# A transformer step with a two-way scan: row transfers by halves, operand loads two items ahead, side jobs in more slots

## The chip, the cores and the metric

The kernel runs on one core of one Trainium2 chip. The metric is device time in microseconds (us) of one execution; a kernel's number is the median of its runs.

## What is computed

One layer on 128 context and 1024 latent tokens, 1024 channels: a half-step SwiGLU FFN, a token mixer, a second half-step FFN, each between norms with modulation. The mixer is what the change touches. Its first branch is a scan over tokens in both directions, for 8 heads of 64 channels:

```python
kk = k_h * p['k_k'].astype(f32).reshape(H, N)
kk = kk * lax.rsqrt(jnp.sum(kk * kk, -1, keepdims=True) + 1e-12)
...
k_d = k_h * (1 + (a_d - 1) * k_a)
...
S = (S * w_t[:, :, None, :]
     + sa[..., None] * (kk_t * a_t)[:, :, None, :]
     + v_t[..., None] * k_t[:, :, None, :])
...
y = y + ((bonus[0] + bonus[1]) * v_h).reshape(B, T, D_RWKV)
y = y * jax.nn.sigmoid(g.astype(f32))
```

The second branch is a gated convolution of width 3. Both are projected, gated, added and projected again.

## The kernel before, in words

Channels lie on the 128 partitions, tokens along the free axis, in three tiles of 384 tokens. A dense product is three matmuls of 128x384 (high and low halves of a split float32), lines L740 to L742, tile `pj`; a projection of 128 output channels over all tokens is 24 products. The mixer has 1056 products.

A pair of heads shares 128 partitions and is called p (0 to 3). Its projections r, k and v, and per direction the decay `sg` and two iclr factors, go to DRAM: `opd`, nine rows per pair, with a view `ops2` of two pairs. What the scan needs of a pair's two heads stands in mirrored rows: `mirrored` (L772) writes or reads head 0 at one row and head 1 at the next, as one transfer whose first dimension is 2. `k_to_dram` stores k so, `stage_k` loads and stores so.

The scan is cut into 18 items: (g, j) with two groups g of two pairs and eight blocks j of 128 tokens for latent tokens, then two items for the context. An item covers block j forwards and block 7 - j backwards. `front` calls `stage_b` once per direction: it loads the decays into `SG` (one buffer per direction) and five operand rows into `ops` (pool `q2`, two buffers), multiplies them on VectorE and GpSimd, and makes the products `scr` (L1043) and `bkt` (L1058) on TensorE. `solve` inverts a triangular matrix, on VectorE for the most part, and ends in the matmuls `l` (L1112). `seq_latent` runs the scan's two steps (`sq`, `yp`).

Beside the items run side jobs in three lanes, at most one step of one of them every second slot: `stage_k` makes kk (matmuls `cps`, `kkb`, `bon`), stores it, and stores the bonus to `bvd`; `stage_v` turns v (`vt`); `finish` ends y (`gv`) and stores it to `yad`. A slot is one dense product; a job says with `yield n` how many slots it lets pass. `PB.first` sets an instruction behind the product of its slot in the scheduler's order. `fill(n)` passes n slots, and `need` passes slots until a job is done. The loop over items is:

```python
            if i + 1 < NI:
                gn, jn = items[i + 1]
                need("kk", *((jn, -1) if gn == 2 else (gn, jn // 2, 3 - jn // 2)))
            with chain():
                if i + 1 < NI:
                    front(i + 1)
                ...
                if i + 1 < NI:
                    solve(A[i + 1], i + 1)
            side(jobs.get(i, ()))
            fill(GI)
```

`chain` gives an item's instructions the highest priority, `beside` gives the side jobs the next, and the products the lowest; from these priorities and its own estimate of times a scheduler sets each engine's order, which the chip then keeps. All transfers but one are issued by SP in order. What waits for kk: item 0 for blocks 0 and 3 of group 0, item 2 for blocks 1 and 2, items 8 and 10 for the same of group 1, items 16 and 17 for the context.

Of the kernel before, what the change touches and what calls it, by code (L numbers as in the profile page):

```python
# [658 lines left out]
def mixer(nc, tc, pool, env):  # L659
# [49 lines left out]
    def store(dst, src):  # L709

        late.append((dst, src, clock["dense"]))
# [59 lines left out]

    def mirrored(p, row, sign, t0, n):  # L772

        t_ = ops2[p // 2]
        ps = 18 * T
        return bass.AP(tensor=t_.tensor, offset=t_.offset + 2 * row * T + p % 2 * T + t0, ap=[[64 * ps + 2 * sign * T, 2], [ps, 64], [1, n]])

    def k_to_dram(p):
        def f(t, ps):
            o = e.tmp("fso", tag="s")  # L780
            PB.first(S.activation(out=o, in_=ps, func=AF.Copy))
            store(mirrored(p, 5, -1, t * TW, TW), o)
        return f

    made = set()
# [14 lines left out]
    with ExitStack() as ph:  # L800
# [15 lines left out]
            G.memset(t_, 0.0)  # L816
        HR = [slice(0, 64), slice(64, 128)]

        GI, GF, GL, GM, GC, SG_ = 40, 8, 16, 6, 14, 2
        def job_g(p):  # L820
            yield from proj(1536 + p * 128, to_dram(gd[p], AF.Tanh, scale=0.5))
            evict()
# [120 lines left out]
        def stage_k(p, t0, n, bon=True):  # L943

            while ("rkv", p) not in made:
                yield 1
            nt = n // 128
            k = q1.tile([128, 256], F32, name="ok", tag="ok")[:, :n]
            PB.first(SP.dma_start(k, mirrored(p, 5, -1, t0, n)))
            r = oload(opd[p][:, 3], t0, n, "or")  # L950
            f0, f1 = (q1.tile([128, 256], F32, name=f"o{x}", tag=f"o{x}")[:, :n] for x in "di")
            SP.dma_start(f0, mirrored(p, 2, -1, t0, n))
            SP.dma_start(f1, mirrored(p, 7, -1, t0, n))
            yield GL
            a = q1.tile([128, 256], F32, name="oa", tag="oa")[:, :n]
            PB.first(S.activation(out=a, in_=k, func=AF.Square, scale=e.KK_[:, p:p + 1]))
            b = f0
            PB.first(V.tensor_tensor(out=b, in0=f0, in1=f1, op=ALU.add))
            V.tensor_tensor(out=b, in0=b, in1=k, op=ALU.mult)
            V.scalar_tensor_tensor(out=b, in0=r, scalar=rk4[:, p:p + 1], in1=b, op0=ALU.mult, op1=ALU.mult)  # L960
            v = r
            SP.dma_start(v, vd[p][:, t0:t0 + n])
            yield 3
            rs = compact(a, nt, sel, 2, 1.0, 1e-12, "oc", PB)
            yield GC
            ps = ps_.tile([128, 256], F32, name="kkb", tag="oc", bufs=1)[:, :n]
            for i in range(nt):
                for h in range(2):
                    PB.matmul(ps[HR[h], i * 128:(i + 1) * 128], rs[:, 2 * i + h:2 * i + h + 1].to_broadcast([128, 64]), ident, start=True, stop=True)
            kk = a  # L970
            V.scalar_tensor_tensor(out=kk, in0=k, scalar=e.KK_[:, p:p + 1], in1=ps, op0=ALU.mult, op1=ALU.mult)
            SP.dma_start(mirrored(p, 4, 1, t0, n), kk)
            made.add(("kk", p, (t0 - NCTX) // 256))
            yield 4
            ps = ps_.tile([128, 256], F32, name="bon", tag="oc", bufs=1)[:, :n]
            PB.matmul(ps, bones, b, start=True, stop=True)
            o = v
            V.tensor_tensor(out=o, in0=v, in1=ps, op=ALU.mult)
            S.activation(out=o, in_=o, func=AF.Identity, bias=gb4[:, p:p + 1])
            SP.dma_start(bvd[p][:, t0:t0 + n], o)  # L980
            yield GF

        def stage_v(p, t0, n, zv):
# [13 lines left out]
                S.activation(out=zv[HR[1 - h], 0:nb, p % 2, HR[h]], in_=ps[HR[1 - h], 0:nb], func=AF.Copy)  # L997
            made.add(("vt", p, (t0 - NCTX) // 256))

        def oload(src, t0, n, tag, first=lambda ins: None):  # L1000
            a = q1.tile([128, 256], F32, name=tag, tag=tag)[:, :n]
            first(SP.dma_start(a, src[:, t0:t0 + n]))
            return a

        def zi(g, b):

            return b if g == 0 else (1, 0, 3, 2)[b]

        def stage_b(g, d, t0, A, it):

            n, nb, s0 = 256, 4, 0
            assert all(("kk", 2 * g + pp, (t0 - NCTX) // 256) in made for pp in range(2))
            ops = q2.tile([128, 5, 256], F32, name="ops", tag="ops")
            sg = SG[d][:, :nb]
            for pp in range(2):
                SP.dma_start(sg[:, 2 * pp:2 * pp + 2, 1:65], ops2[g][:, 8 * d, pp, t0:t0 + 128].rearrange("p (s t) -> p s t", t=64))
            SP.dma_start(ops.rearrange("p k (i t) -> p k i t", i=2), ops2[g][:, 1 + 2 * d:6 + 2 * d, :, t0:t0 + 128])
            X, r, kw = (ops[:, 0:2], ops[:, 2], ops[:, 3:5]) if d == 0 else (ops[:, 3:5], ops[:, 0], ops[:, 1:3])
            c3 = "p (s t) -> p s t"
            Fd = q1.tile([128, 4, 65], F32, name="ff", tag="ff")[:, :nb]  # L1020
# [176 lines left out]
        def item_bufs():  # L1197
            ab = [s2.tile([128, 2, 4, 128], F32, name=f"ab{d}", tag=f"AB{d}") for d in range(2)]
            return {"N": q1.tile([128, 2, 4, 32], F32, name="nn", tag="nn"), "T": [t_[:, 0] for t_ in ab], "BT": [t_[:, 1] for t_ in ab],
                    "FT": [s2.tile([128, 4], F32, name=f"ft{d}", tag=f"FT{d}") for d in range(2)],  # L1200
                    "E": [s2.tile([128, 4, 2, 128], F32, name=f"e{d}", tag=f"S{d}") for d in range(2)]}

        def finish(p, t0, n, y):
            while ("g", p) not in made:
                yield 1
            nt = n // 128
            bv = oload(bvd[p], t0, n, "f1", PB.first)
            tg = oload(gd[p], t0, n, "f2", PB.first)
            yc = q1.tile([128, 256], F32, name="yc_", tag="f3")[:, :n]
            yo = y  # L1210
            if t0 < NCTX:
                ps = ps_.tile([128, 256], F32, name="gm", tag="oc", bufs=1)[:, :n]
                PB.matmul(ps, bones, y, start=True, stop=True)
                V.scalar_tensor_tensor(out=yc, in0=ps, scalar=-1.0 / 64, in1=y, op0=ALU.mult, op1=ALU.add)
                yo = yc
            a = q1.tile([128, 256], F32, name="ysq", tag="f4")[:, :n]
            PB.first(S.activation(out=a, in_=yo, func=AF.Square))
            yield GM
            rs = compact(a, nt, sel, 2, 1.0 / 64, 64e-5, "oc", PB)
            yield GC  # L1220
            ps = ps_.tile([128, 256], F32, name="gv", tag="oc", bufs=1)[:, :n]
            for i in range(nt):
                for h in range(2):
                    PB.matmul(ps[HR[h], i * 128:(i + 1) * 128], rs[:, 2 * i + h:2 * i + h + 1].to_broadcast([128, 64]), ident, start=True, stop=True)
            V.tensor_tensor(out=yc, in0=yo, in1=ps, op=ALU.mult)
            V.scalar_tensor_tensor(out=yc, in0=yc, scalar=gg4[:, p:p + 1], in1=bv, op0=ALU.mult, op1=ALU.add)
            o = tg
            V.scalar_tensor_tensor(out=o, in0=tg, scalar=1.0, in1=yc, op0=ALU.add, op1=ALU.mult)
            SP.dma_start(yad[p][:, t0:t0 + n], o)
            made.add(("y", p, (t0 - NCTX) // 256))  # L1230

        def init_state(p, A):
# [87 lines left out]

        def front(i):
            g, j = items[i]
            A[i] = item_bufs()
            if g < 2:
                stage_b(g, 0, NCTX + j * 128, A[i], i)
                stage_b(g, 1, NCTX + (7 - j) * 128, A[i], i)
            else:
                for d in range(2):
                    stage_b(j, d, 0, A[i], i)
# [71 lines left out]
        def beside():  # L1401
            return tc.high_priority(offset=39000)

        side(ks(0, 0, 3) + vs(0, 0, 3))
        need("kk", 0, 0, 3)
        with chain():
# [2 lines left out]
        for i, (g, j) in enumerate(items):  # L1409
            if g == 1 and j in (0, 2):  # L1410
                need("y", 0, *((1, 2), (0, 3))[j // 2])
            if g < 2 and j in (0, 2):
                need("vt", g, *((0, 3), (1, 2))[j // 2])
            if g == 2:
                need("vt", j, -1)
                need("y", 1, *((1,), (2,))[j])
            if i + 1 < NI:
                gn, jn = items[i + 1]
                need("kk", *((jn, -1) if gn == 2 else (gn, jn // 2, 3 - jn // 2)))
            with chain():  # L1420
                if i + 1 < NI:
                    front(i + 1)
                if g < 2:
                    seq_latent(g, j, A[i], A.get(i + 1) if j < 7 else None)
                else:
                    seq_ctx(j, A[i])
                if i + 1 < NI:
                    solve(A[i + 1], i + 1)
            side(jobs.get(i, ()))
            fill(GI)  # L1430
        while any(l.cur for l in lanes.values()):
            fill(1)

# [85 lines left out]
```

## Time and profile before

| | us |
|---|---|
| median of 3 runs | 3277.09 |
| lowest, highest | 3270.9, 3281.26 |
| the profiled execution | 3285.59 |
| its span, first to last instruction | 3283.8 |
| PE busy | 3023.5 (92%) |
| VectorE (DVE) busy | 1817.5 (55%) |
| ScalarE (ACT) busy | 1150.9 (35%) |
| GpSimd (POOL) busy | 454.6 (14%) |
| bytes moved by DMA | 330.78 MB, 101 GB/s over the span |

The span in 40 slices of 82 us, in tenths; the mixer lies in slices 12 to 27:

```profile
PE   8999999999989878888889898769989999999998
DVE  7535665565875244557674667766683233323356
PEclk9999999999989988988999889869999999999999
```

A row names engine, tile and line. "Idle before" is the time that the engine had nothing to do before the instruction, and behind the arrow stands what ended it. PEclk is the granted clock of TensorE as a share of 2.4 GHz; it has two levels, 1.2 and 2.4 GHz, so 0.75 over a stretch means that half of it ran at 1.2.

### The profile page before, as it was taken

The page shows a single profiled execution, that of the slowest core. Times are in us where ns is not written, and L with a number is a line of the kernel's source. Part 1 is how long each engine was busy: PE and PEld are TensorE (multiplying, and loading weights), DVE is VectorE, ACT ScalarE, POOL GpSimd, SP SyncE. Part 2 cuts the span into 40 slices and gives each one's busy share as a digit, 9 for nine tenths or more (in the row PEclk, how much of TensorE's full clock was granted, in tenths as well). Part 3 has the DMA queues.
Part 4 walks back from the last instruction along what each step waited for, and adds up shares of the span by engine and source line. Part 5 has one row for each costly group of instructions (what it writes and reads, how often), then busy time and mean ns, then how long its engine had stood idle before and what let it go on. Part 6 is the DMA issues. An engine that isn't in the chain of part 4 may idle for free.

```text
span 3283.8 us, 54891 instructions
## 1 busy us (share of the span) xinstructions
PE 3023.5 (92%) x21284; PEld 2850.2 (87%) x21284; DVE 1817.5 (55%) x4148; ACT 1150.9 (35%) x2618; POOL 454.6 (14%) x436
## 2 busy tenths in 40 slices
PE   8999999999989878888889898769989999999998
PEld 5999999999888867767777777649989999999998
DVE  7535665565875244557674667766683233323356
ACT  5421111114546224344544444422554211121244
POOL 1000000000240121333331323200120000000012
PEclk9999999999989988988999889869999999999999
DMA  8423333325534331322232333225532111111244
GB/s 270 144 63 95 97 102 87 86 85 153 157 109 162 125 118 58 110 76 78 81 111 84 98 87 98 85 78 157 178 104 87 36 46 43 44 39 42 82 144 132
DMA packets 481137, 330.78 MB, mean 101 GB/s; under 512 B 47008, under 2 KB 458988, under 8 KB 480876
## 3 DMA queue, kind: packets, MB, share of 16 engines
q1 hardware_dynamic: 480248, 326.79, 33.4%
q8 instruction: 167, 2.74, 0.3%
q14 instruction: 94, 0.77, 0.1%
q10 hardware_dynamic: 308, 0.44, 0.0%
q0 software_dynamic: 320, 0.04, 0.0%
HBM read 265.58 MB, written 61.60 MB: 100 GB/s over the span
## 4 chain that ended last, share of the span: by engine, by line
PE 68%; DVE 17%; DMA 6%; ACT 4%; issue 3%; POOL 1%; SPq 0%; DVEq 0%; ACTq 0%; POOLq 0%
PE po L220 6%; PE po L219 6%; PE po L221 6%; PE pg L220 5%; PE pg L219 5%; PE pg L221 5%; PE pu L220 5%; PE pu L219 5%; PE pu L221 5%; PE pj L740 3%; PE pj L742 2%; PE pj L741 2%; DVE un L1084 2%; PE scr L1043 2%; DMA ops<-opd 2%
## 5 line engine op out<-in xcount | busy, mean ns | idle before, releaser
L138 ACT ACTIVATE whi<-wst 128x512 fp32r<-128x512 f32 (+1 forms) x578 | 350.4, 611 | 753.1 <-PE po L221 392.8
L139 DVE TENSOR_TENSOR wlo<-wst,whi 128x512 fp32r<-128x512 f32 (+1 forms) x480 | 326.6, 681 | 305.2 <-ACT whi L138 295.7
L740 PE MATMUL pj<-hh,wlo 128*128 128x384 f32 x1056 | 382.2, 362 | 0.3 <-ACT fso L768 0.3
L741 PE MATMUL pj<-hl,whi 128*128 128x384 f32 x1056 | 372.7, 353 | 2.7 <-POOL hl L269 1.4
L742 PE MATMUL pj<-hh,whi 128*128 128x384 f32 x1056 | 374.6, 355 | 0.0
L219 PE MATMUL po<-ah,wlo 128*128 128x384 f32 x1056 | 357.1, 339 | 4.0 <-ACT ah L138 4.0
L220 PE MATMUL pg<-hl,whi 128*128 128x384 f32 x1056 | 356.1, 337 | 4.9 <-POOL hl L269 2.9
L219 PE MATMUL pg<-hh,wlo 128*128 128x384 f32 x1056 | 357.4, 338 | 1.7 <-DVE wlo L139 1.3
L220 PE MATMUL po<-al,whi 128*128 128x384 f32 x1056 | 356.3, 338 | 0.4 <-DVE al L139 0.4
L221 PE MATMUL po<-ah,whi 128*128 128x384 f32 x1056 | 355.7, 337 | 0.0
L221 PE MATMUL pg<-hh,whi 128*128 128x384 f32 x1056 | 355.5, 337 | 0.0
L219 PE MATMUL pu<-hh,wlo 128*128 128x384 f32 x1056 | 355.2, 336 | 0.0
L220 PE MATMUL pu<-hl,whi 128*128 128x384 f32 x1056 | 353.8, 335 | 0.0
L221 PE MATMUL pu<-hh,whi 128*128 128x384 f32 x1056 | 353.8, 335 | 0.0
L279 POOL TENSOR_TENSOR ss<-ss,sqt 128x384 f32<-128x384 f32 x78 | 88.7, 1140 | 1697.0 <-ACT sqt L278 1534.9
L432 DVE TENSOR_TENSOR sil<-sil,pu 128x384 f32<-128x384 f32 x132 | 72.9, 552 | 353.8 <-PE pu L221 353.6
L404 DVE TENSOR_TENSOR o<-o,po 128x384 f32<-128x384 f32 x288 | 159.2, 553 | 172.0 <-PE po L221 170.8
L740 PEld LDWEIGHTS pj<-hh,wlo 128*128 128x128 f32 x1056 | 206.4, 195 | 12.5 <-issue 7.0
L741 PEld LDWEIGHTS pj<-hl,whi 128*128 128x128 f32 x1056 | 207.1, 196 | 8.6 <-issue 2.2
L742 PEld LDWEIGHTS pj<-hh,whi 128*128 128x128 f32 x1056 | 206.9, 196 | 7.6 <-issue 3.7
L220 PEld LDWEIGHTS pg<-hl,whi 128*128 128x128 f32 x1056 | 199.9, 189 | 7.0 <-POOL hl L269 3.8
L219 PEld LDWEIGHTS po<-ah,wlo 128*128 128x128 f32 x1056 | 198.6, 188 | 5.0 <-ACT ah L138 5.0
(584 smaller groups left out, 5763.9 us busy)
## 6 DMA issues: line engine op xcount, KB each, us to landing
wst<-in_ffn_w SPq DMA_DIRECT2D x324, 256.0 KB
wmod<-in_w_mod SPq DMA_DIRECT2D x144, 256.0 KB
wst<-in_w_in SPq DMA_DIRECT2D x94, 256.0 KB
ops<-opd SPq DMA_DIRECT2D x36, 640.0 KB
wst<-in_ffn_w SPq DMA_DIRECT2D x96, 192.0 KB
xo<-xd SPq DMA_DIRECT2D x64, 192.0 KB
wst<-in_w_out SPq DMA_DIRECT2D x48, 256.0 KB
opd<-zv SPq DMA_DIRECT2D x24, 384.0 KB
```

Source lines behind the costliest of these rows:

```text
L138: first(S.activation(out=hi, in_=src, func=AF.Copy))
L139: eng.tensor_tensor(out=lo, in0=src, in1=hi.bitcast(F32), op=ALU.subtract)
L219: PE.matmul(ps, lo, xh, start=(k == 0), stop=False)
L220: PE.matmul(ps, hi, xl, start=False, stop=False)
L221: later.tick(PE.matmul(ps, hi, xh, start=False, stop=(k == nk - 1)))
L279: eng.tensor_tensor(out=ssum, in0=ssum, in1=q, op=ALU.add)
L404: V.tensor_tensor(out=O[m][t], in0=O[m][t], in1=ps, op=ALU.add)
L432: V.tensor_tensor(out=s, in0=s, in1=pu, op=ALU.mult)
L740: PE.matmul(ps, lo, xh, start=(k == 0), stop=False)
L741: PE.matmul(ps, hi, xl, start=False, stop=False)
L742: ins = PE.matmul(ps, hi, xh, start=False, stop=(k == 7))
L1043: PE.matmul(ps[64 * o:64 * o + 64, i], BK[64 * h:64 * h + 64, o, i * 64:i * 64 + 64], E[64 * h:64 * h + 64, s0 + i, h], start=True, stop=True)
```

## The change

Four edits. `mirrored` gives two transfers of 64 rows, and its users issue both. `stage_k` marks its loads and stores with the product of their slot, and passes slots in other places: 4 before kk's store, 4 before the bonus's, where it passed 4 in one place, so 49 in all instead of 45; `finish` passes 4 before its store. The operand loads move from `stage_b` to `operands(i)`, which is called for item i + 2 after 16 of the 40 slots of item i, if kk is there by then, and from `front` otherwise. The slots of `fill(GI)` become `GO` = 16 and the rest.

```diff
     def mirrored(p, row, sign, t0, n):
 
-        t_ = ops2[p // 2]
-        ps = 18 * T
-        return bass.AP(tensor=t_.tensor, offset=t_.offset + 2 * row * T + p % 2 * T + t0, ap=[[64 * ps + 2 * sign * T, 2], [ps, 64], [1, n]])
+        return [opd[p][64 * h:64 * h + 64, row + sign * h, t0:t0 + n] for h in range(2)]
...
-            store(mirrored(p, 5, -1, t * TW, TW), o)
+            for h, dst in enumerate(mirrored(p, 5, -1, t * TW, TW)):
+                store(dst, o[64 * h:64 * h + 64])
...
-            PB.first(SP.dma_start(k, mirrored(p, 5, -1, t0, n)))
-            r = oload(opd[p][:, 3], t0, n, "or")
+            turned(k, mirrored(p, 5, -1, t0, n), PB.first)
+            r = oload(opd[p][:, 3], t0, n, "or", PB.first)
...
-            SP.dma_start(f0, mirrored(p, 2, -1, t0, n))
-            SP.dma_start(f1, mirrored(p, 7, -1, t0, n))
+            turned(f0, mirrored(p, 2, -1, t0, n), PB.first)
+            turned(f1, mirrored(p, 7, -1, t0, n), PB.first)
...
-            SP.dma_start(v, vd[p][:, t0:t0 + n])
+            PB.first(SP.dma_start(v, vd[p][:, t0:t0 + n]))
...
-            SP.dma_start(mirrored(p, 4, 1, t0, n), kk)
+            yield 4
+            for h, dst in enumerate(mirrored(p, 4, 1, t0, n)):
+                PB.first(SP.dma_start(dst, kk[HR[h]]))
             made.add(("kk", p, (t0 - NCTX) // 256))
-            yield 4
...
-            SP.dma_start(bvd[p][:, t0:t0 + n], o)
+            yield 4
+            PB.first(SP.dma_start(bvd[p][:, t0:t0 + n], o))
             yield GF
...
+        def turned(dst, srcs, first=lambda ins: None):
+            for h, src in enumerate(srcs):
+                first(SP.dma_start(dst[HR[h]], src))
...
+        def operands(i, first=lambda ins: None):
+
+            g, j = items[i]
+            for d in range(2):
+                gg, t0 = (g, NCTX + (j, 7 - j)[d] * 128) if g < 2 else (j, 0)
...
+                ops = q2.tile([128, 5, 256], F32, name="ops", tag="ops")
+                for pp in range(2):
+                    first(SP.dma_start(SG[d][:, 2 * pp:2 * pp + 2, 1:65], ops2[gg][:, 8 * d, pp, t0:t0 + 128].rearrange("p (s t) -> p s t", t=64)))
+                first(SP.dma_start(ops.rearrange("p k (i t) -> p k i t", i=2), ops2[gg][:, 1 + 2 * d:6 + 2 * d, :, t0:t0 + 128]))
+                OPS[i, d] = ops
...
-            SP.dma_start(yad[p][:, t0:t0 + n], o)
+            yield 4
+            PB.first(SP.dma_start(yad[p][:, t0:t0 + n], o))
...
+            if (i, 0) not in OPS:
+                operands(i)
...
-            fill(GI)
+            fill(GO)
+            if i + 2 < NI and all(("kk", 2 * kks(i + 2)[0] + pp, b) in made for b in kks(i + 2)[1:] for pp in range(2)):
+                with chain():
+                    operands(i + 2, PB.first)
+            fill(GI - GO)
```

How the order of instructions moves, first on SP at item 0, first direction: kk's store (`opd<-oa`) and the operand load behind it (`ops<-opd`), before:

```order
L972 DMA opd_110<-oa 2x64x256
L716 DMA opd_111<-fso 2x64x384
L952 DMA od<-opd_110 128x1x256
L1017 DMA ops<-opd_110 128x10x128
L980 DMA bvd_117<-or 128x256
L716 DMA vd_114<-fso 128x384
```

and now:

```order
L716 DMA vd_114<-fso 128x384
L973 DMA opd_110<-oa 64x256 x2
L981 DMA bvd_117<-or 128x256
L1025 DMA ops<-opd_110 128x10x128
L151 DMA wst<-in_w_in 128x4x128 x2
L716 DMA vd_114<-fso 128x384
```

The load `od` of the next job has left the place between store and operand load, and the bonus's store `bvd` stands there instead.

Second, on PE, the end of the dense products. The tiles `ab_20235` belong to item 14, `ab_20513` to item 15, `e_21095` to item 16. Before, the last product is followed by the scan of items 15 and 16:

```order
L740 MATMUL pj<-hh_2_9400,wlo 128x384
L741 MATMUL pj<-hl_2_9401,whi 128x384
L742 MATMUL pj<-hh_2_9400,whi 128x384
L1182 MATMUL yp<-ab_20513,zv_9434 64x64 x4
L1182 MATMUL yp<-ab_20514,zv_9433 64x64 x4
L1173 MATMUL yp<-e_21095,zv_9432 64x64 x4
L1173 MATMUL yp<-e_21096,zv_9432 64x64 x4
```

and now by the solve of item 14:

```order
L740 MATMUL pj<-hh_2_9402,wlo 128x384
L741 MATMUL pj<-hl_2_9403,whi 128x384
L742 MATMUL pj<-hh_2_9402,whi 128x384
L177 MATMUL gv<-cst,ny 64x128 x4
L177 MATMUL cps<-cst,ysq 128x2 x2
L177 MATMUL vt<-cst,lv 64x64 x4
L1127 MATMUL l_20515<-xr,ab_20235 32x32 x2
L1127 MATMUL l_20515<-xr,ab_20236 32x32 x2
```

The number of products is the same; they stand earlier, ahead of the fronts that wait for kk.

## Rows read from the trace of the kernel before

**Rows 1.** Stretches of the mixer, early and last: length, busy time, PEclk, DMA share, GB/s.

```profile
core 0: us, PE busy (x) PEld busy (x) DVE busy (x) ACT busy (x) POOL busy (x), PEclk, DMA share, GB/s
1080.00:1202.00 122.00, 96.64 (x609) 91.12 (x609) 26.52 (x61) 26.66 (x58) 24.87 (x19) 0.88 0.35 108
2098.00:2200.00 102.00, 56.82 (x671) 43.90 (x671) 68.68 (x265) 29.16 (x88) 7.35 (x12) 0.60 0.16 46
```

**Rows 2.** Timeline of PE, nine gaps: start, length, instruction [idle before <- what ended it].

```profile
1107.59 0.37 PE L177 MATMUL cps<-cst,oa 128*128 128x2 f32 x1 [9.08 <-ACT oa L956]
...
1163.61 0.48 PE L1043 MATMUL scr<-e,ops 64*64 64x128 f32 x2 [9.38 <-DVE ops L1032]
...
1201.89 0.48 PE L1043 MATMUL scr<-e,ops 64*64 64x128 f32 x2 [6.90 <-DVE ops L1032]
...
1275.15 0.44 PE L177 MATMUL vt<-cent,lv 64*64 64x64 f32 x3 [6.21 <-DMA lv<-vd]
...
1336.31 0.48 PE L1043 MATMUL scr<-e,ops 64*64 64x128 f32 x2 [4.90 <-DVE e L1036]
...
1373.68 0.48 PE L1043 MATMUL scr<-e,ops 64*64 64x128 f32 x2 [5.59 <-DVE ops L1032]
...
1609.66 0.32 PE L1112 MATMUL l<-xr,ab 32*32 32x32 f32 x4 [6.79 <-DVE nt L231]
...
1769.46 0.44 PE L1043 MATMUL scr<-e,ops 64*64 64x128 f32 x4 [3.77 <-DVE ops L1032]
...
1810.37 0.48 PE L1043 MATMUL scr<-e,ops 64*64 64x128 f32 x2 [5.13 <-DVE ops L1032]
```

**Rows 3.** The chain that ended last: start, length, transfer of kk, operands, a plain one.

```profile
1146.38 6.22 DMA opd<-oa
1152.62 8.49 DMA ops<-opd
...
1755.90 4.87 DMA opd<-oa
...
1802.98 4.89 DMA ops<-opd
...
2181.97 1.83 DMA f<-bvd
```

**Rows 4.** A stretch with kk's store of item 0, second direction, in flight.

```profile
1188.00:1191.50 3.50, 3.50 (x21) 3.45 (x20) 0.42 (x1) 1.97 (x4) 0.37 (x1) 1.00 0.13 39
```

**Rows 5.** Who waited for whom: us in total, times, longest us.

```profile
DVE od L958 <- DMA od<-opd: 28.8, 7, 6.2
```

**Rows 6.** Ten us behind a gap's end, the first and the last of nine.

```profile
1107.60:1117.60 10.00, 10.00 (x48) 9.75 (x49) 2.53 (x11) 1.33 (x3) 2.12 (x2) 0.78 0.52 159
...
1609.70:1619.70 10.00, 9.80 (x158) 7.61 (x158) 5.08 (x14) 5.54 (x16) 2.58 (x5) 0.80 0.22 66
```

**Rows 7.** Transfers of `opd` on SP, plain and two-headed: issue time ns min/median/max.

```profile
L1002 SPq DMA_DIRECT2D or<-opd x20: 319/329/464, 935.3 to 2014.7; - x20
L949 SPq DMA_DIRECT2D ok<-opd x20: 492/504/745, 952.1 to 1992.2; - x20
```

**Rows 8.** The chain: fronts of items 14, 16, 17, scans of items 16 and 17.

```profile
1982.46 1.90 PE scr L1043 x16
...
2077.58 1.90 PE scr L1043 x16
...
2116.45 1.05 PE sq L1161 x16
2117.75 1.90 PE scr L1043 x16
...
2155.02 1.05 PE sq L1161 x16
```

**Rows 9.** Timeline of SP: the operand load of item 14, first direction.

```profile
1942.06 0.37 SPq L1017 DMA_DIRECT2D ops<-opd  x1
```

**Rows 10.** Timeline of PE, the last matmul of two products in a row.

```profile
1079.77 0.33 PE L742 MATMUL pj<-hh,whi 128*128 128x384 f32 x1
...
1080.29 0.34 PE L742 MATMUL pj<-hh,whi 128*128 128x384 f32 x1
```

More of the change, by code (lines that the diff above doesn't have):

```diff
@@ L817, in mixer @@
         HR = [slice(0, 64), slice(64, 128)]
-        GI, GF, GL, GM, GC, SG_ = 40, 8, 16, 6, 14, 2
+        GI, GO, GF, GL, GM, GC, SG_ = 40, 16, 8, 16, 6, 14, 2
         def job_g(p):
@@ L1007, in zi @@
             return b if g == 0 else (1, 0, 3, 2)[b]
+        OPS = {}
+        def operands(i, first=lambda ins: None):
+            g, j = items[i]
+            for d in range(2):
+                gg, t0 = (g, NCTX + (j, 7 - j)[d] * 128) if g < 2 else (j, 0)
+                assert all(("kk", 2 * gg + pp, (t0 - NCTX) // 256) in made for pp in range(2))
+                ops = q2.tile([128, 5, 256], F32, name="ops", tag="ops")
[3 more added lines that the diff above has]
+                OPS[i, d] = ops
         def stage_b(g, d, t0, A, it):
             n, nb, s0 = 256, 4, 0
-            assert all(("kk", 2 * g + pp, (t0 - NCTX) // 256) in made for pp in range(2))
-            ops = q2.tile([128, 5, 256], F32, name="ops", tag="ops")
+            ops = OPS.pop((it, d))
             sg = SG[d][:, :nb]
-            for pp in range(2):
-                SP.dma_start(sg[:, 2 * pp:2 * pp + 2, 1:65], ops2[g][:, 8 * d, pp, t0:t0 + 128].rearrange("p (s t) -> p s t", t=64))
-            SP.dma_start(ops.rearrange("p k (i t) -> p k i t", i=2), ops2[g][:, 1 + 2 * d:6 + 2 * d, :, t0:t0 + 128])
             X, r, kw = (ops[:, 0:2], ops[:, 2], ops[:, 3:5]) if d == 0 else (ops[:, 3:5], ops[:, 0], ops[:, 1:3])
@@ L1402, in beside, with kks @@
             return tc.high_priority(offset=39000)
+        def kks(i):
+            g, j = items[i]
+            return (j, -1) if g == 2 else (g, j // 2, 3 - j // 2)
         side(ks(0, 0, 3) + vs(0, 0, 3))
@@ L1418, in mixer @@
                 gn, jn = items[i + 1]
-                need("kk", *((jn, -1) if gn == 2 else (gn, jn // 2, 3 - jn // 2)))
+                need("kk", *kks(i + 1))
             with chain():
```

## The prediction

> **What bounds the kernel now.** I read the page first, then the program in stages, then the idle time of TensorE (PE) in the mixer, then what released it. Outside the mixer PE works almost without a break, and the change touches nothing there. Inside it, PE is the bound while products `pj` stand beside the scan items, and two kinds of loss are to be seen.
>
> The first is gaps. Between 1080 and 1202 us PE was busy for 96.6 of 122 us at a granted clock of 0.88 of full [rows 1]. Nine gaps of the mixer end at a wait that has a transfer behind it [rows 2]: six at `scr`, the first matmul that needs the operands `ops` of item 0, 2 or 10 (9.38, 6.90, 4.90, 5.59, 3.77 and 5.13 us, in sum 35.7); one at `cps` of a side job (9.08), one at `vt` (6.21), one at `l` of a solve (6.79). Together 57.8 us. Item 0, 2 and 10 are those whose front has to wait for a fresh `kk`: VectorE makes kk, a store brings it to DRAM, a load brings it back among the operands, and PE stands in order behind it. The chain of waits shows this as pairs [rows 3]: the store of kk took 6.22 us and the load behind it 8.49 at item 0; other stores took down to 4.87, other loads down to 4.89. A plain transfer of the same 128 KB took 1.83 us in the last row there. The store is two-headed, that is its rows go to two places of DRAM by head; while one was in flight the 16 DMA engines were busy for 0.13 of their time at 39 GB/s [rows 4], about two engines' worth. The Trainium skill says why, in "DMA: Bandwidth & Descriptors", section "Why a DMA increments its semaphore by 16 and not by 1": a copy is spread over the largest number of engines up to 16 that divides the slowest dimension of both sides, which for two heads is 2. The share in the row agrees.
>
> The `l` gap belongs here too: VectorE, which makes the solve, waited for two-headed loads (28.8 us in seven waits for `od`, the longest 6.2) [rows 5], and the solve stood behind.
>
> The second loss is the clock. Behind each of the nine gaps PE ran part of the time at 1.2 instead of 2.4 GHz. In the 10 us after the restart the granted clock was 0.78 in the first and 0.80 in the last case [rows 6]; over the nine, the missing share adds up to 24.2 us.
>
> **The change part by part.**
>
> *Two-headed transfers become two of 64 rows.* 92 transfers (12 stores of k, 60 loads, 20 stores of kk) become 184 halves. Issuing costs 0.50 us for a two-headed one and 0.33 for a plain one [rows 7], so each pair adds 0.16 us to SP's queue, 15 us over more than 1000, beside everything. How long a half takes no row shows; the bounds are a plain transfer of the same row length (1.83 us) and the undivided one (4.87 to 6.22) [rows 3]. I take 2 us, since a half has 64 rows to share as the plain one has 128. The store of `bvd`, which stood behind the operand load, now stands ahead of it and waits for ScalarE, about 0.9 us later than the halves land; so 2.9 us from kk to the load instead of 4.87 to 6.22. The load itself I put at 5.0, near its shortest, since the two engines that it shared with the two-headed ones are free again. With three more products (1.6 us) between kk and `scr`, a site gains 3.5 to 8.4 us. The gap of 9.38, whose store and load were the slowest, closes to 1.0; that of 6.90, whose two were short, keeps about 3; the others keep 1 or less. I leave 7 of 35.7: **28.7 us back**.
>
> The other three: `cps` waited for a load `ok` and for weights that lay behind two-headed transfers; 8 of 9.08 back. `vt` waited for a load that followed two-headed ones; 3.2 of 6.21. `l`: 5 of 6.79. Together 16.2, and **45 us of idle time** in all. Of the 24.2 us of slow clock I take two thirds, **16 us**, since some of the work behind a gap is small chain matmuls, and some short gap may still lower the clock.
>
> *Operands two items ahead.* In a middle item they were early already: item 14's first load was issued at 1942.06 us and its `scr` ran at 1982.46 [rows 8, 9]. Two buffers serve the two directions, so the load still has to wait for the front of the item before, and the instruction order has it behind that front in both kernels. For items 0, 1, 2 and 10 kk is not made in time and the load stays in the front. Cost and gain: nothing; what hides the loads is the 40 us up to `scr`.
>
> *Side jobs' transfers in their turn.* `stage_k` now passes 49 slots of one product instead of 45. Three stretches of the program wait for its kk, and products fill them. Counted in PE's order, the products ahead of `scr` go from 257 to 272 for item 0's second direction, then to item 2's from 180 to 196 more, and from item 8 to item 10's from 124 to 155 more: 15 + 16 + 31 = 62 products earlier. A product is 0.52 us (two `L742` rows one product apart) [rows 10]: **32 us added** to stretches in which PE is the bound. They are missing at the end: the last product now stands ahead of item 14's solve instead of amid item 16. What an item is worth with and without products: 95.1 us for two items with 40 and 43 [rows 8], 40.2 with 13, and 38.6 from scan to scan with none [rows 8]. So a product beside an item costs only about 0.2 us, since the item's own chain through PE, VectorE and GpSimd takes 38.6 anyway. Items 14 to 16 should take about 45 + 38.6 + 38.6 = 122 instead of 135.3: 13 us back. From that I take 6, because four `finish` jobs that ran beside products now fall into the bare end, where VectorE was busy for 68.7 of 102 us [rows 1]: **7 us back**.
>
> Sum: -45 - 16 + 32 - 7 = **-36 us**. The profiled execution took 3285.6 us, so 3249.6; it stands 8.5 us above the median of 3277.1, so I predict a median of 3241 us.
>
> **The rivals.** About 0.3% (10 us) is what a measurement of this kernel can tell from no change, so "same" is 3267 to 3287.
>
> *More comes back.* All nine gaps and the slow clock go: -57.8 - 24.2 + 32 - 13 = -63, so 3214. For it: besides the gaps, VectorE's waits of rows 5 stand inside items. Against: the residue of 3 us at item 0's second direction follows from durations that the change leaves alone.
>
> *The halves pay a fixed time each.* If they land one after the other, a store takes 2 x 1.83 = 3.7 us instead of 2, each of the six sites keeps 1.7 us more, 10 us, and some of the slow clock stays, 5: -21, so 3256. The Trainium skill speaks for it in "DMA: Bandwidth & Descriptors", section "Bandwidth": transfers under 64 KB are dominated by their descriptors, and it wants large ones; a half is 64 KB. No row shows two such halves. I give it little, since the second is issued 0.33 us behind the first [rows 7].
>
> *The split does nothing.* If the two-headed transfer is slow for its scattered rows and not for its two engines, only the 1.6 us of three more products per site come back, 10 us, some clock, 5, and 7 at the end, against 32: +10, so 3287, just on the far side of no change; with a little help in the waits of VectorE it reads as none.
>
> *Slower.* SP issues in order, and the store of `bvd` now stands between kk's store and the operand load. It waits for `bon` on PE, then for VectorE and ScalarE. In the trace the load was issued 4.9 to 6.2 us after kk's store [rows 3]. If `bvd` is ready only 6 us after that store, the six gaps stay as they are and the slots are paid for: +32 - 7 - 16 - 8 (half the clock) = +1. It is slower in earnest from 7.5 us on; at 10 us, with VectorE amid a solve's chain, each gap grows by 4: +25, so 3302. For it: the order shows that place. Against: at these sites PE itself stood idle, and what `bvd` waits for follows kk's own matmul by four products, 2 us.
>
> **How the numbers follow.** The forecast 0.52, more comes back 0.17, fixed time each 0.08, the split does nothing 0.10, slower 0.13. The forecast's own spread is from 3220 to 3262 (residues 0 or 3 us per gap, clock 10 to 24 us). Faster by more than 0.3%: the forecast, more and fixed time, less a share for the forecast's edge: 0.73. Same: most of "does nothing" and that edge, 0.13. Slower: 0.14. The range goes from 3208, a little under "more", to 3288, which leaves out the slower case and a rest below, under 2 in 10.
>
> **What would show it.** Right: kk's halves land within 2 to 3 us, the operand load behind them in about 5; the six gaps at `scr` at 3 us or less in sum 7; no gap of 9 us at `cps`; the granted clock from 1080 to 1202 us of the mixer well over 0.88; the last product `pj` ahead of the solve of item 14, and items 15 to 17 at 38 to 40 us each. Wrong: halves that take over 4 us; gaps at `scr` as before with SP at the `bvd` store ahead of the load; bare items well over 40 us; new gaps at `vt`, `kkb` or `gv`.

## The result, and the profile after

| | before | changed |
|---|---|---|
| median | 3277.81 us (4 runs) | 3250.85 us (4 runs) |
| lowest, highest | 3270.9, 3281.26 | 3247.96, 3256.03 |
| profiled execution, its span | 3285.59, 3283.8 | 3247.96, 3245.9 |

The ratio is 0.9922, with a 95% interval from 0.9902 to 0.9943: 27 us less, 19 to 32 by the interval. Forecast were 36 us less than 3277, with 3208 to 3288 as the range. The two profiled executions differ by 38 us, because that of before was the longest of its runs and that of the change the shortest; so differences of places in the two traces are some 11 us too favourable in all, and I give medians where there are any.

First the page of the changed kernel: busy tenths of PE and the granted clock, in 40 slices of 81 us.

```profile
PE   8999999999989999898899886569989999999998
PEclk9999999999989999998999997669989999999999
```

Against the strips of before, three slices of PE early in the mixer (the 14th to the 16th) have risen from 8, 7 and 8 to 9, and three late ones, the last items, stand at 6, 5 and 6, with the clock at 7, 6 and 6. Both show in two stretches (start and end, length, busy time of PE, PEld, DVE, ACT, POOL, PEclk, DMA share, GB/s):

```profile
1080.00:1182.00 102.00, 100.04 (x659) 95.30 (x657) 22.86 (x61) 27.77 (x60) 24.55 (x19) 1.00 0.45 131
...
2055.00:2160.00 105.00, 55.50 (x657) 43.83 (x657) 65.68 (x252) 26.46 (x82) 7.36 (x12) 0.57 0.10 29
```

The first answers to [rows 1]: from 1080 us to item 0's second `scr` it now takes 102 us instead of 122, PE is busy for all but 2 of them, and the clock is full. The gaps of [rows 2] at `scr`, at the same six places, on the timeline of PE:

```profile
1150.03 0.44 PE L1058 MATMUL scr<-e,ops 64*64 64x128 f32 x4 [1.00 <-DVE ops L1047]
...
1181.29 0.43 PE L1058 MATMUL scr<-e,ops 64*64 64x128 f32 x4 [0.96 <-DVE ops L1047]
...
1309.17 0.44 PE L1058 MATMUL scr<-e,ops 64*64 64x128 f32 x4 [1.22 <-DVE ops L1047]
...
1345.29 0.44 PE L1058 MATMUL scr<-e,ops 64*64 64x128 f32 x4 [2.39 <-DVE ops L1047]
...
1744.76 0.43 PE L1058 MATMUL scr<-e,ops 64*64 64x128 f32 x4 [1.08 <-DVE ops L1047]
...
1778.90 0.44 PE L1058 MATMUL scr<-e,ops 64*64 64x128 f32 x4 [0.86 <-DVE ops L1047]
```

In sum 7.5 us instead of 35.7. What stands behind it, first on SP's timeline at item 0, second direction (start, issue time, transfer):

```profile
1170.59 1.35 SPq L973 DMA_DIRECT2D opd<-oa  x2
1173.70 0.34 SPq L981 DMA_DIRECT2D bvd<-or  x1
1174.15 1.12 SPq L1025 DMA_DIRECT2D ops<-opd  x2
```

then the lines of kk's halves and of the operand load (issue time ns min/median/max, then the time to landing):

```profile
L973 SPq DMA_DIRECT2D opd<-oa x40: 445/528/1212, 1081.9 to 2016.0; - x40
...
DMA to landing us min/median/max: 1.8/2.0/3.4
...
L1025 SPq DMA_DIRECT2D ops<-opd x36: 359/368/656, 1142.9 to 2042.5; - x36
...
DMA to landing us min/median/max: 4.2/4.7/6.7
```

A half lands in 2.0 us (median), where the whole took 4.87 and 6.22 [rows 3]; the load behind it starts 3.6 us after kk's store, with `bvd` between them, and takes 4.7. While each of the two halves of 1170.59 us was in flight, the stretches (columns as above) were these:

```profile
1171.70:1172.20 0.50, 0.50 (x5) 0.50 (x4) 0.00 (x0) 0.07 (x1) 0.00 (x0) 1.00 0.53 127
1172.60:1173.10 0.50, 0.50 (x5) 0.50 (x4) 0.39 (x1) 0.00 (x0) 0.00 (x0) 1.00 0.54 129
```

A DMA share of 0.53 and 0.54 at 127 and 129 GB/s stands against 0.13 at 39 GB/s for the undivided store [rows 4].

The end of the mixer is the other side. The chain that ended last, with the fronts of items 14 to 17 and item 17's scan, as in [rows 8]:

```profile
1938.44 1.78 PE scr L1058 x16
...
1989.00 1.90 PE scr L1058 x16
...
2033.18 1.90 PE scr L1058 x16
...
2075.28 1.90 PE scr L1058 x16
...
2111.34 1.05 PE sq L1176 x16
```

From scr to scr 50.6, 44.2 and 42.1 us, where I had 45, 38.6 and 38.6. Item 14 is reached 44 us earlier than before (1982.46 us there), and the scan of item 17 also 44 (2155.02): nothing was won on that last stretch.

### The profile page after: what moved, and what is told of

It is laid out like the page before. It is cut to its first block, busy times and chain, and to the rows that moved or that the text cites. A ratio compares the mean times of both kernels' runs of the same rounds, so it can differ in the third digit from the quotient of the medians.

```text
span 3245.9 us, 55035 instructions
## 1 busy us (share of the span) xinstructions
PE 3005.2 (93%) x21284; PEld 2841.4 (88%) x21284; DVE 1817.3 (56%) x4148; ACT 1148.8 (35%) x2618; POOL 454.2 (14%) x436
## 5 line engine op out<-in xcount | busy, mean ns | idle before, releaser
L219 PEld LDWEIGHTS pg<-hh,wlo 128*128 128x128 f32 x1056 | 200.3, 190 | 2.6 <-DVE wlo L139 1.6
```

What stands on the lines that cost most here:

```text
L219: PE.matmul(ps, lo, xh, start=(k == 0), stop=False)
```

## The experiments

The theory at the start, called A in the expectations: the split makes the gain; the new slots draw products forward and cost about 31 us; the bare end gives nothing back. "Marks" are the calls of `PB.first` on the side jobs' transfers. Differences are each median against the median of before on the same chip, brackets the 95% interval of the ratio.

| run | median us | against before |
|---|---|---|
| the change | 3250.85 | -27.0, 0.9922 [0.9902, 0.9943] |
| e1: split alone | 3229.47 | -46.3, 0.9854 [0.9836, 0.9873] |
| e8: split of kk's store alone | 3253.90 | -20.1, 0.9940 [0.9925, 0.9956] |
| e9: split of the loads alone | 3241.52 | -32.4, 0.9897 [0.9879, 0.9916] |
| e10: split and marks | 3217.01 | -60.2, 0.9819 [0.9796, 0.9842] |
| e4: the change without its slots | 3209.84 | -66.0, 0.9796 [0.9777, 0.9816] |
| e5: the change, no operands ahead | 3246.71 | -29.1, 0.9911 [0.9892, 0.9930] |
| e3: the change without the split | 3285.38 | +9.6, 1.0029 [1.0019, 1.0039] |
| e12: the change, 48 products more | 3244.68 | -32.5, 0.9902 [0.9884, 0.9920] |
| e11: before, 12 slots for loads | 3225.27 | -52.0, 0.9838 [0.9815, 0.9861] |
| f12: e4, 12 slots for loads | 3152.54 | -121.4, 0.9626 [0.9608, 0.9643] |
| f8: e4, 8 slots for loads | 3154.43 | -119.5, 0.9622 [0.9600, 0.9645] |

### The parts of the change

e1 makes in the kernel before only those edits of the diff that split transfers.

> The kernel before with the split alone: slots, marks and operand loads as before. Theory A (the split gives the whole gain; the four more slots per kk job cost about 31 us of products drawn forward, and the bare items at the end give nothing of it back): the split is worth 27 + 31 = 58, less 1.6 us at each of six scr sites for the three products that are missing, so 3222 us (3210 to 3234), below the changed kernel by 15 us or more; scr gaps of 1 to 4 us, last product beside item 16. Rival B (the halves only pay with the new slots and marks, which bring kk's store and the load behind it forward in SP's order): gaps of 3 us or more stay at scr, 3250 to 3268 us. Rival C (a good part of the gain is the operand loads two items ahead): 3250 or more, with the gaps at scr closed.

3229: theory A. Alone, the split is worth more than the whole change. The six gaps at `scr` come to 15.6 us in its trace, against 35.7 before and 7.5 in the change; so the split alone does not close them as far as the change does.

e3 is the change with two-headed transfers again:

```diff
-            for h, dst in enumerate(mirrored(p, 4, 1, t0, n)):
-                PB.first(SP.dma_start(dst, kk[HR[h]]))
+            PB.first(SP.dma_start(mirrored(p, 4, 1, t0, n), kk))
```

and the same for the other users of `mirrored`.

> The changed kernel with two-headed transfers again, so slots, marks and operand loads as in the change. Theory A: +31 for the products drawn forward, 1.6 us back at each of six sites and a little of the clock, so 3277 + 31 - 15 = 3293 us (3283 to 3303), slower than before. Rival B (slots and marks make the gain): 3250 to 3265 us. Rival C (operand loads make part of it): 3268 to 3280 us.

3285, slower than before: theory A again, in the lower half of its range. Slots, marks and operand loads together lose.

e4 undoes the slots alone:

```diff
-            yield 4
             for h, dst in enumerate(mirrored(p, 4, 1, t0, n)):
                 PB.first(SP.dma_start(dst, kk[HR[h]]))
             made.add(("kk", p, (t0 - NCTX) // 256))
+            yield 4
...
-            yield 4
             PB.first(SP.dma_start(bvd[p][:, t0:t0 + n], o))
...
-            yield 4
             PB.first(SP.dma_start(yad[p][:, t0:t0 + n], o))
```

> The changed kernel with the slots as before (four behind kk's store, none more ahead of the stores of kk, bvd and yad); split, marks and operand loads stay. Theory A: the products stand about where they stood before, so 3251 - 31 + 10 (three products less at six sites) = 3230 us at most and 3215 at best, 3222 as the middle. Rival B: the gaps come back in part, 3245 us or more. Rival D (the tail's loss is the bare items' own chain and lanes, whatever stands earlier): 3240 to 3251 us, with items 15 to 17 at 42 to 50 us each though products stand beside them.

3210, more than theory A wanted: the slots cost 66.0 - 27.0 = 39 us. They also close something: without them the six gaps at `scr` are 12.3 us in sum, with them 7.5. One sign of rival D is there (items 14 and 15 take 48.0 and 45.0 us, though products stand beside them), but its time is not.

e5 leaves out the call of `operands(i + 2, ...)`, so that every front loads its own.

> The changed kernel with every operand load in its front, as before; split, slots and marks stay. Theory A: 3251 us, within 6 us either way. Rival C: the loads two items ahead carry 10 us or more of the gain, so 3261 us or more, with PE waiting at scr in middle items.

3247, as theory A had it. e10 is e4 without that call:

> The kernel before with the split and the marks on the side jobs' transfers; slots as before, every operand load in its front. It stands between the split alone (3229 us) and the run without new slots (3210 us). Theory M (the marks make the 20 us between them: a transfer no longer stands behind others that the scheduler thought earlier): 3204 to 3216 us. Rival C (the operand loads two items ahead make them): 3223 to 3235 us.

3217, just above the range of theory M and well below that of C. From e1 to e10 there are some 14 us, though the two intervals just overlap. The marks make them, or the one other thing that differs: in e10 a front issues the operand loads of both directions at its start, in e1 those of the second direction behind the first one's work; no run parts the two. From e10 to e4 the loads ahead are worth 6 us, inside the intervals, and in the change itself (e5) they cost 2. So the loads ahead show no effect. One thing that the marks do is to be seen on SP's timeline at item 0, second direction, first of e1:

```profile
1167.18 1.10 SPq L972 DMA_DIRECT2D opd<-oa  x2
1169.31 1.10 SPq L1002 DMA_DIRECT2D od<-opd  x2
1170.52 1.36 SPq L1021 DMA_DIRECT2D ops<-opd  x2
```

and of e10:

```profile
1163.27 1.11 SPq L972 DMA_DIRECT2D opd<-oa  x2
...
1165.88 1.05 SPq L1024 DMA_DIRECT2D ops<-opd  x2
```

The `od` load of the next job no longer stands between kk's store and the operand load, which is issued 2.6 us behind the store instead of 3.3 and lands 4.4 us later instead of 6.0; the gap at `scr` there is 0.9 us instead of 4.6. Over the six sites the gaps go from 15.6 to 12.7 us only, so most of the 14 us arises elsewhere and is not traced.

### Store or loads

e8 splits kk's store in the kernel before, e9 the loads of k, f0 and f1. The 12 stores of k stay undivided in both.

> The kernel before with the store of kk alone as two halves; the loads of k, f0, f1 and the store of k stay two-headed. Theory A: it carries the six gaps at scr and their slow clock, about 30 of the 46 us that the whole split is worth in the kernel before, so 3246 us (3238 to 3254); the gap at cps (9 us) stays. Rival F (the loads carry most, since two-headed loads hold up whatever shares their two engines): 3256 us or more.

> The kernel before with the loads of k, f0 and f1 alone as two halves each; the stores of kk and k stay two-headed. Theory A: the gaps at cps, vt and l and their clock, some 16 of 46 us, so 3260 us (3252 to 3268), with the gaps at scr as before. Rival F: 3246 us or less, the gaps at scr smaller too.

3254 and 3242: the larger part is the loads', as rival F had it, and theory A was wrong on this. The two add up to 52 us, the whole split gives 46, so they overlap little. The timeline of PE shows what each closes; e8, `cps` of the side job and the `scr` of item 0:

```profile
1104.01 1.01 PE L177 MATMUL cps<-cst,oa 128*128 128x2 f32 x4 [8.82 <-ACT oa L958]
...
1158.11 0.69 PE L1046 MATMUL scr<-e,ops 64*64 64x128 f32 x4 [7.03 <-DVE ops L1035]
...
1193.26 0.43 PE L1046 MATMUL scr<-e,ops 64*64 64x128 f32 x4 [4.22 <-DVE ops L1035]
```

and e9:

```profile
1101.05 0.61 PE L177 MATMUL cps<-cst,oa 128*128 128x2 f32 x4 [0.45 <-ACT oa L958]
...
1152.06 0.69 PE L1049 MATMUL scr<-e,ops 64*64 64x128 f32 x4 [6.37 <-DVE ops L1038]
...
1189.32 0.69 PE L1049 MATMUL scr<-e,ops 64*64 64x128 f32 x4 [5.91 <-DVE ops L1038]
```

With the store alone, the gap at `cps` stays at 8.8 us and those at `scr` shrink from 9.38 and 6.90 to 7.03 and 4.22; with the loads alone, `cps` closes, and the `scr` gaps shrink to 6.37 and 5.91 although their own store is as before. So part of these gaps is not the store's but the slow loads'; by which way the loads lengthen them (on SP, or on the DMA engines) no run parts. Over all six sites the gaps are 26.4 us in e8 and 28.7 in e9, against 35.7 before and 15.6 with both (e1). The waits of VectorE for the loads (us in total, times, longest) are in e8

```profile
DVE od L961 <- DMA ok<-opd: 24.0, 3, 10.8
DVE od L960 <- DMA od<-opd: 22.0, 6, 5.9
```

and in e9

```profile
DVE od L961 <- DMA ok<-opd: 13.5, 3, 5.6
DVE od L960 <- DMA od<-opd: 9.4, 4, 3.1
```

so half of them is left when the loads are split.

### What a product costs, early and at the end

Slots move products between two places: stretches that wait for kk, and the last items. The length of the last items, from item 14's first `scr` to item 17's first scan, against PE's work in it (columns as above); before, the change, e4, e12 and f12:

```profile
1982.40:2154.90 172.50, 134.20 (x1680) 113.11 (x1678) 125.14 (x419) 77.85 (x225) 39.99 (x44) 0.85 0.29 86
```

```profile
1938.40:2111.30 172.90, 104.56 (x1471) 85.83 (x1470) 120.96 (x404) 71.29 (x212) 33.26 (x38) 0.72 0.22 62
...
1988.90:2033.10 44.20, 24.29 (x372) 19.66 (x370) 34.10 (x118) 20.18 (x65) 9.36 (x10) 0.65 0.25 74
```

```profile
1905.20:2074.30 169.10, 130.29 (x1668) 109.86 (x1667) 127.15 (x419) 78.76 (x226) 41.65 (x44) 0.85 0.30 87
```

```profile
1940.30:2109.10 168.80, 122.27 (x1616) 102.75 (x1614) 122.14 (x404) 77.06 (x222) 37.74 (x42) 0.82 0.28 80
...
1983.40:2029.80 46.40, 39.71 (x486) 33.75 (x484) 38.08 (x122) 26.84 (x78) 11.49 (x12) 0.98 0.45 125
2029.80:2073.50 43.70, 22.76 (x328) 18.98 (x326) 26.00 (x91) 12.43 (x36) 8.69 (x10) 0.58 0.21 61
```

```profile
1845.40:2015.80 170.40, 156.30 (x1885) 134.95 (x1884) 128.14 (x417) 84.53 (x241) 49.80 (x50) 0.98 0.34 98
```

Five kernels, PE's work from 104.6 to 156.3 us, and the length stays between 168.8 and 172.9. Where products are missing, the granted clock falls instead: 0.72 in the change, 0.98 in f12. The second rows of the change and of e12 are the stretch of item 15: 44.2 us with PE busy for 24.3 at a clock of 0.65, and 46.4 with 39.7 at 0.98; the third of e12 is item 16. e12 puts that to the test with 48 products more at the end (the last gate is computed twice, into the same place):

```diff
-            for m in range(8):
+            for m in (0, 1, 2, 3, 4, 5, 6, 7, 7):
                 yield from job_gate(m)
```

> The changed kernel with 48 products more at the end of the mixer (the last gate's two projections made a second time, into the same place). PE's work grows by 48 x 0.52 = 25 us. Theory A (beside the bare last items a product costs nothing, since PE waits there anyway and its work keeps the clock up): 3251 us, within 7 either way, with the granted clock of items 15 and 16 back at 0.9 and more. Rival H (0.2 us a product, as the prediction reckoned): 3260 us. Rival I (full price): 3270 us or more.

3245, though 48 products at 0.52 us are 25 us of work. All of them stand in items 14 and 15; PE's busy time in the whole stretch grows by 17.7 us only, since at the higher clock the items' own matmuls take less of it. Item 15's clock was 0.98 as theory A had it, but item 16's, where the products had run out, was 0.58 and not 0.9. A product beside these items costs nothing on balance; what it takes and what the better clock gives back are not measured apart.

Then the other side: `GL` is the number of slots between a side job's loads and their first use, 16 in both kernels.

```diff
-        GI, GO, GF, GL, GM, GC, SG_ = 40, 16, 8, 16, 6, 14, 2
+        GI, GO, GF, GL, GM, GC, SG_ = 40, 16, 8, 12, 6, 14, 2
```

> The changed kernel without the new slots (as the run at 3210 us), and with 12 instead of 16 slots between a side job's loads and their use. Theory A (a product drawn forward costs 0.52 us, one beside the last items costs nothing): by PE's order 48 products more stand behind item 16's front, so 3210 - 25 = 3185 us (3178 to 3195). Rival G (the loads need the slots): waits of 2 us and more at cps, 3200 us or more.

> As the run with 12 slots, with 8. Theory A: 86 products more than at 16 stand behind item 16's front; the last items have room for about 56 of them, the rest runs at its full price behind them, so nothing more than at 12 is to be had: 3175 to 3192 us. Rival G: 8 slots (4.2 us) are too short for loads that queue behind others, so waits at cps, kkb and vt, and 3195 us or more.

3153 and 3154. Theory A had the sign and that 8 slots bring nothing beyond 12, but it was 30 us short, so a product drawn forward did not cost its 0.52 us alone. By PE's order 80 products fewer stand ahead of item 10's second `scr` than in e4 (729 and 809); at 0.52 us that is 42 of 55 us. The rest arose between items 2 and 10, and I have not separated it. f12 is the fastest version here, with f8 level, 94 us below the change by the differences; its page shows PE and clock without a hole in the mixer:

```profile
PE   8999999999988999998899989889899999999998
...
PEclk9999999999999999999999999999999999999999
```

e11 asks whether that needs the split: before, with 12 for 16.

> The kernel before with 12 instead of 16 slots between a side job's loads and their use, two-headed transfers as they are. By PE's order 71 products more stand behind item 10's first scr. Theory A (products alone count, at the 0.7 us apiece that the runs with 12 slots gave): 3274 - 50 = 3224, less what the slow loads give back at cps, so 3215 to 3240 us. Rival G (two-headed loads don't land within 12 slots, 6.2 us, so fewer slots pay only with the split): waits at cps of 2 us and more at most jobs, 3250 us or more.

3225, within 2 us of theory A's first sum, and waits as rival G had them are there all the same, three at `cps` with 3.9, 4.4 and 4.2 us, two of them here on PE's timeline:

```profile
1100.27 1.01 PE L177 MATMUL cps<-cst,oa 128*128 128x2 f32 x4 [3.87 <-ACT oa L956]
...
1267.57 1.01 PE L177 MATMUL cps<-cst,oa 128*128 128x2 f32 x4 [4.39 <-ACT oa L956]
```

Four slots fewer per job are worth more than these. The gains of e11 (52 us) and of e4 (66 us) add up to 118, and f12 has 121: faster transfers and fewer slots are two separate gains.

## Why the prediction was right, step by step

The time, the sign and the mechanism of the split held; two terms of the sum were off, in opposite directions, and a third was left out. That the sum came so close is in part luck.

**The split, -45 of idle time and -16 of clock.** Right in its mechanism: a half lands in 2.0 us, as I took it; 3.6 us from kk's store to the operand load where I had 2.9; 4.7 for the load where I had 5.0; 7.5 us left at six `scr` where I had 7. That a two-headed transfer is slow for using two engines fits the share of 0.13 with one in flight [rows 4], the 0.53 and 0.54 with a half in flight, and halves that are over twice as fast; e1 and e3 show that splitting is what pays. The size was too high: alone the split gave 46, not 61. Part of that is the forecast's own book-keeping: it counted under the split what the three more products per site close, 1.6 us at each of six sites, and e1 has none of these. Of the 28.7 us that I promised at the six sites, the split alone closed 35.7 - 15.6 = 20. Its parts were put wrongly, too. I gave the store 28.7 of 45 us of idle time and the loads 16; measured, slow clock included, the loads give 32 and the store 20, and at the six `scr` the store alone closed only 9 us.

**The marks.** I counted them at nothing, as part of the slots. They, with the order of loads in the front, are worth some 14 us by e1 and e10; a load that no longer stands ahead of the operands on SP is one part of it, the rest is open. So everything but the slots came to 66 us (e4) where the forecast had 61: a term that I left out covers the one that I put too high.

**Operands two items ahead, nothing.** Right: -6 and +2 in two settings, both within the intervals.

**The slots, +32 and -7.** The first half was right: the change reaches item 14 at 1938.4 us, e4 at 1905.2, 33 us for 62 products, with the 5 us that the slots close at the six `scr` already taken off. The second half is the step that failed. "Items 14 to 16 should take about 45 + 38.6 + 38.6 = 122 instead of 135.3" - they took 50.6 + 44.2 + 42.1 = 137. I took the 38.6 of a bare item from the last two scans [rows 8], which are those of context items. Item 15 is a latent one, and three `finish` jobs end beside it. VectorE's rows of L1205, the sums of the scan's state (stretch, length, busy time and count, PEclk, DMA share, GB/s), for item 15 and item 16 of the change:

```profile
1988.90:2033.10 44.20, 3.83 (x16) 0.65 0.25 74
2033.10:2075.20 42.10, 1.88 (x8) 0.66 0.15 42
```

Twice as many in item 15; and of L1243, the end of a `finish`, it has three, item 16 one.

Besides, I charged 0.2 us for each product that was beside these items, and e12 shows such products to be free: taking them away had nothing to give. What PE lost there was the clock, 0.65, so that the item's own small matmuls ran for the most part at 1.2 GHz. That this and the jobs make up the 44.2 us between them is argued, not shown, and e12 speaks against the clock as the cause: at 0.98, with products beside it, item 15 took 46.4 us. What the five kernels show is that these items take about as long with products as without. From the last scan to the end of the span the change takes 1134.6 us and e4 1128.2, six more. They arise at once: the next stage's first matmul `pb` starts 43.9 us behind the last scan in the change (2111.34) and 36.3 in e4 (2074.3),

```profile
2155.23 0.67 PE L219 MATMUL pb<-brb02h,wlo 128*128 128x384 f32 x1
...
2110.59 0.67 PE L219 MATMUL pb<-brb02h,wlo 128*128 128x384 f32 x1
```

since more `finish` jobs of the context are left over there: behind the `cps` of 2138.36 us PE does three `gv`, 5.5 us apart, where e4 has one behind the same `cps` (2104.67). So the slots cost 39 us (31 by e10 and e5) instead of 25.

In sum -66 + 39 = -27 against -61 + 25 = -36.

**The rivals.** "More comes back" (3214) is not what the change does, but nearly what e4 does. "A fixed time each, one after the other" fell with the 2.0 us. The Trainium skill, in "DMA: Bandwidth & Descriptors", section "Bandwidth", calls transfers under 64 KB descriptor-dominated and wants large ones. Here the pieces of 64 KB were the faster ones, at a DMA share of 0.53 against 0.13 for the undivided store; between transfers that keep equally many engines busy, no run here weighs that rule. "The split does nothing" was priced at 3287; e3, where there is no split, took 3285. "Slower", by `bvd` between store and load, would have begun in earnest at 7.5 us; with `bvd` and all, 3.6 passed. Of my signs of being wrong two came, both in the bare end: items well over 40 us, and gaps at `gv` of 5.8 and 4.1 us, where before had one of 4.0.

Wrong in a small thing: the issue time of a half is 0.53 us, not the 0.33 of a plain transfer, so a pair costs SP twice what one two-headed transfer did. No run shows what that cost.

## What to carry to other kernels

Look at how many DMA engines a transfer can use before asking where to issue it: halves landed in 2.0 us where one transfer with a first dimension of 2 took 4.9 to 6.2, and splitting the loads (32 us) paid more than splitting the store that the operands visibly wait for (20 us). When filler work covers latencies, ask of every wait how much of it the filler must pass, and where the filler will be missing: here a product that had to pass before a stretch could start cost its full time and more (0.53 us each in the change, 0.7 in f12), and one beside the last items cost nothing. Price a stretch without filler from one that has no filler and the same jobs, at the clock it will have.

## What the runs showed of the hardware that I had not expected

A stretch bound by a chain of small matmuls and VectorE work kept its length (168.8 to 172.9 us) while PE's work in it grew by half, and the granted clock rose with that work from 0.72 to 0.98. And a transfer of 64 rows took SP longer to issue than one of 128. In the changed kernel a `bvd` store of 128 rows took 0.33 us after a pause of SP and 0.45 right behind another transfer (medians of 13 and 7); a half of kk's store took 0.47 after a pause, and its partner right behind it 0.59 (medians of 20). The two-headed ones took 0.50 [rows 7].
